# A macaron encoder layer: scale vectors of three RMS norms spread into PSUM by transposes, and the late norms moved to VectorE

## The chip, the cores and the metric

One core of one Trainium2 chip. The time is that of one execution on the device in microseconds; the number to predict is the median of several runs. A core has TensorE (matmul, "PE"), VectorE ("DVE"), ScalarE ("ACT"), GpSimd ("POOL") and SyncE ("SP", which here only issues DMAs). TensorE writes its results into PSUM, which has eight banks of 128 x 512 float32. VectorE and ScalarE read PSUM too. Each engine works through its own queue in order.

## The reference

One layer on x of 1024 tokens by 1024 channels, float32. An RMS norm multiplies each token by a number of its own and each channel by a learned scale vector (the "gain"):

```
x = x + 0.5 * swiglu(rms_norm(x, ffn1_norm), ffn1_wg, ffn1_wu, ffn1_wd)
x = x + hybrid_mixer(rms_norm(x, mix_norm), ...)      # Fourier branch and differential attention, gated
x = x + 0.5 * swiglu(rms_norm(x, ffn2_norm), ffn2_wg, ffn2_wu, ffn2_wd)
return rms_norm(x, final_norm)

rms_norm(x, g) = x * rsqrt(mean(x * x, over channels) + eps) * g
swiglu(x, wg, wu, wd) = (silu(x @ wg) * (x @ wu)) @ wd
```

## The kernel before

Tokens are cut into eight tiles of 128, t = 0 to 7; a tile is kept as two pieces of 128 tokens x 512 channels. Every float32 product is made of three reduced-precision ones, for which each operand is split in a high part (ScalarE, L133) and a low part (VectorE or GpSimd, L134). The large products use a seven-product scheme on 2 x 2 blocks (`seven_products`, L370): for each block of output columns TensorE runs seven products of twelve matmuls (L386) into two "p" banks of PSUM, ScalarE copies a product out (L398), VectorE adds another to the copy (L402). The weights of these products are loaded by SP into `r2` tiles, summed by GpSimd (L217) and split (L133, L134).

Each of the three norms feeds such products, so the normalized tokens must be turned (channels onto partitions), summed for the scheme, and split:

- `norm_tile` (L349) multiplies the two pieces of a tile in place by the token number r (a column) and the gain (128 x 512, the same row on every partition). One VectorE instruction does both products of a piece (L358). With `spread` the first piece goes another way: ScalarE multiplies by r (L355), GpSimd by the gain (L356).
- Two tiles make a pair. `pair_blocks` (L305) appends six steps to the list `blocks`: `first` turns two pieces (eight 128 x 128 transposes on TensorE, L295, into two "b" banks), `second` and `third` one piece each into one bank, with copies, sums (L312, L326, L334, L335) and splits of what lies in the banks; the three others split sums in SBUF. A bank is free again after the last of its readers.
- The gains are loaded by `load_gain` (L265): two DMAs, each of which reads 512 numbers and writes them onto 128 partitions, into two pieces of the store "x".

PSUM is dealt out as four "b" banks and four "p" banks. `bank()` takes the next "b" bank in turn; where `bank_list` holds banks, it deals those in rotation.

Where the norms run:

- Start (first norm): x is loaded tile by tile, with the gain's DMAs behind tile 1. Tiles 0 to 3 are normalized at once and their two pairs mostly turned before the first product. Tiles 4 to 7 come later: `each1` (L1131) is called after each of the first fourteen products, which work on tokens of tiles 0 to 3 alone (256 columns); its calls 4 to 7 normalize a tile each, the last two with `spread`, and each call takes one step (two from call 7 on) from `blocks` (`drain`).
- The second norm: the down projection before it (`Lower.run`) ends with the sums for tiles 4 to 7. Tiles 0 to 3 are normalized in `tail` (L624), while these products run, with banks that they leave free. `late` (L659) is called after each of the first fourteen products of the mixer (`project`); in its calls 1 to 4 it normalizes tiles 4 to 7, all with `spread`, by `done1`.
- The third norm: the same with `done2`, before the second feed-forward (`ffn`, with `each2`).

The order in each engine's queue is set when the program is built: a planner simulates the program with its own costs (`schedule_with_timeline_sim`, L2011) and places what is ready by program order; instructions marked `in_order` (in `norm_tile` from tile 4 on) are kept in program order.

Of the kernel before, what the change touches and what calls it, by code (L numbers as in the profile page):

```python
# [10 lines left out]
F32 = mybir.dt.float32  # L11
F32R = mybir.dt.float32r
I32 = mybir.dt.int32
AF = mybir.ActivationFunctionType
ALU = mybir.AluOpType
# [4 lines left out]
P = 128  # L20
S = 1024
D = 1024
DT = D // P
# [11 lines left out]
NP = NF // 2  # L35
SPILL = 5
# [12 lines left out]
def encoder_layer(ctx: ExitStack, tc: tile.TileContext, a: dict, out: bass.AP):  # L49
    nc = tc.nc  # L50
    pe, act, dve, pool, sp = nc.tensor, nc.scalar, nc.vector, nc.gpsimd, nc.sync

    cst = ctx.enter_context(tc.tile_pool(name="cst", bufs=1))
    big = ctx.enter_context(tc.tile_pool(name="big", bufs=1))
    dram = ctx.enter_context(tc.tile_pool(name="dram", bufs=1, space=DRAM))
    psum = [None]
# [13 lines left out]
    bank_list = []  # L70

    def bank(tag="b"):
        if bank_list:
            bank_list.append(bank_list.pop(0))
            return bank_list[-1]
        tag = tag if tag in banks else "b"
        return T(psum[0], tag, [P, 512], F32, banks[tag])
# [7 lines left out]
    def r2(shape=None, dt=F32):  # L85
        return T(big, "r2", shape or [P, 512], dt, 14)
# [20 lines left out]
    def give(piece):  # L107
        store[piece[0]].append(piece[1])
# [14 lines left out]
    ident = cst.tile([P, P], F32, name="ident")  # L123
# [132 lines left out]
    def drain(n, skip=()):  # L256
        while n > 0:
            due = [e for e in blocks if e[0] not in skip][:1]
            if not due:
                return  # L260
            blocks.remove(due[0])
            due[0][1]()
            n -= 1

    def load_gain(src):  # L265
        g = [take("x"), take("x")]
        for k in range(2):
            sp.dma_start(out=g[k][1],
                         in_=src[k * 512:(k + 1) * 512].rearrange("(o d) -> o d", o=1).broadcast_to([P, 512]))
        return g  # L270

    def squares(ss, k, xts, junk):

        for i, xt in enumerate(xts):
            src = xt if len(junk.shape) == 2 else xt.rearrange("p (j c) -> p j c", j=4)
            act.activation(junk, src, AF.Square, accum_out=ss[:, 4 * k + i:4 * k + i + 1])
# [69 lines left out]
    half_pair = {}  # L346
    few = [True]

    def norm_tile(t, x, gain, r, spread=False):  # L349

        for k in range(2):
            y = x[k][1]
            keep = in_order if t >= 4 else lambda ins: ins
            if spread and k == 0:
                act.activation(y, y, AF.Copy, scale=r)  # L355
                keep(pool.tensor_tensor(out=y, in0=y, in1=gain[k][1], op=ALU.mult))  # L356
            else:
                keep(dve.scalar_tensor_tensor(out=y, in0=y, scalar=r, in1=gain[k][1], op0=ALU.mult, op1=ALU.mult))  # L358
        half_pair[t] = x
        if t % 2 == 0:  # L360
            return
        pair_blocks(t // 2, half_pair.pop(t - 1), half_pair.pop(t))
# [261 lines left out]
    def tail(low, done):  # L624

        drains = DRAINS[len(low.units)]
        ss, r, turns = [], [], [0]
        few[0] = not low.spills

        def halves(t0, k):  # L630
            return [low.tile(t)[k][1] for t in range(t0, t0 + 4)]

        def hook(q, j, other):
            n = 2 - NBLK + q
            if n == -1 and j == 0:
                done(None, None, None)
                ss.extend((col(8), col(8)))
                low.ss = ss[1]
                ss.append(take("x"))
                squares(ss[0], 1, halves(0, 1), ss[2][1])  # L640
                act.activation(root, ss[0][:, 4:5], AF.Sqrt)
            if n < 0:
                return
            if n == 0 and j == 0:
                squares(ss[0], 0, halves(0, 0), ss[2][1])
                r.extend(rscale(ss[0]))
            if n == 1 and j == 1:
                squares(ss[1], 0, halves(4, 0), ss[2][1])
                give(ss[2])
            bank_list[:] = other[turns[0]:] + other[:turns[0]]  # L650
            if n == 0 and j < 4:
                done(j, low.tile(j), r[j])
            if (n, j) in drains:
                drain(drains[n, j], (T4,))
            turns[0] = other.index(bank_list[0])
            bank_list.clear()
        return hook

    def late(low, done):  # L659

        n, r = [0], []

        def hook():
            n[0] += 1
            if n[0] == 1:
                squares(low.ss, 1, [low.tile(t)[1][1] for t in range(4, TT)], spare(B11))
                r.extend(rscale(low.ss))
            if 1 <= n[0] <= 4:
                t = 3 + n[0]
                done(t, low.tile(t), r[t - 4])  # L670
            drain(1 if n[0] <= 4 else 2)
        return hook


# [23 lines left out]
    sums_d = {k: dram.tile([n, 4, P, 512], F32, name=f"sums{k}_d") for k, n in ((1, NP), (2, NP), ("o", 4))}  # L698

    def down(k, j):  # L700

        f = [a[f"ffn{k}_wd"][t * P:(t + 1) * P, :] for t in (j, j + NP)]
        return [f[i // 2][:, (i % 2) * 512:(i % 2) * 512 + 512] for i in range(4)]
# [9 lines left out]
    def right_sums(jobs):  # L713

        sub = ALU.subtract
        for blks, dst in jobs:
            two = [T(big, "kx", [P, 2, 512], F32, 2) for _ in range(2)]
            b = [t[:, q, :] for t in two for q in range(2)]
            for i in (1, 0, 3, 2):
                in_order(sp.dma_start(out=b[i], in_=blks[i]))  # L720
            for _ in range(4):
                yield
            t3 = rh()
            for n, (o, x, y) in enumerate(((t3, b[3], b[1]), (b[1], b[1], b[0]), (b[3], b[3], b[1]), (b[2], b[2], b[3]))):
                in_order(dve.tensor_tensor(out=o, in0=x, in1=y, op=sub))
                if n % 2 == 1:
                    yield
            for n, o in enumerate((b[1], b[3], t3, b[2])):
                in_order(sp.dma_start(out=dst[n], in_=o))
            yield  # L730
            yield
# [200 lines left out]
    x2_d = dram.tile([S, D], F32, name="x2_d")  # L932
# [160 lines left out]
    keep = {}  # L1093
# [13 lines left out]
    x0 = []  # L1107
    for t in range(TT):
        x0.append([take("h" if t < 4 else "x") for _ in range(2)])
        for k in range(2):  # L1110
            sp.dma_start(out=x0[t][k][1], in_=a["x"][t * P:(t + 1) * P, k * 512:(k + 1) * 512])
        if t == 1:
            gain = load_gain(a["ffn1_norm"])
        elif t == 3:
            ws.ahead(3, 0)
    for t in range(4):
        ss = col(2)
        for k in range(2):
            act.activation(bank(), x0[t][k][1], AF.Square, accum_out=ss[:, k:k + 1])
        r = rscale(ss)[0]  # L1120
        norm_tile(t, x0[t], gain, r)
        if t == 2:
            drain(1)
    drain(6)
    ss = col(8)
    for k in range(2):
        squares(ss, k, [x0[t][k][1] for t in range(4, TT)], spare(B22))
    r4 = rscale(ss)
    hooks = [0]

    def each1():  # L1131
        n = hooks[0]
        hooks[0] += 1
        if 4 <= n <= 7:
            norm_tile(n, x0[n], gain, r4[n - 4], n >= 6)
        if n == 7:
            for g in gain:
                give(g)
        drain(1 if n < 7 else 2)

    low = ffn(1, a["x"], each1, right_sums([(down(1, j), sums_d[1][j]) for j in (*range(SPILL, NP), *range(SPILL))]
                                           + [(outward(j), sums_d["o"][j]) for j in range(4)]), bias_prepare(), mixer_weights())
    state = {}

    def done1(t, x, r):
        if t is None:
            state["gain"] = load_gain(a["mix_norm"])
            ws.open()
            ws.ahead(ws.used + 3, ws.used)
            return  # L1150
        if t == 0:
            new_xn()
        for k in range(2):
            act.dma_start(out=x1_d[t * P:(t + 1) * P, k * 512:(k + 1) * 512], in_=x[k][1])
        norm_tile(t, x, state["gain"], r, t >= 4)

    low.run(tail(low, done1))

# [28 lines left out]
            project((h, 4 + h), None, cols, hook)  # L1189
        hook = None  # L1190
    assert not blocks
    for g in state["gain"]:
        give(g)
    rv = bias_general()
    psum_pool.__exit__(None, None, None)
    psum_pool = tc.tile_pool(name="psum2", bufs=1, space=PSUM, reuse_waits="tile")
# [629 lines left out]
    for n_, (dm, hh) in enumerate(todo):  # L1826
# [8 lines left out]
        y, gb = ready[n_]  # L1835
# [23 lines left out]
    def done2(t, x, r):  # L1859
        if t is None:  # L1860
            state["gain"] = load_gain(a["ffn2_norm"])
            ws.open()
            ws.ahead(ws.used + 3, ws.used)
            return
        if t == 0:
            new_xn()
        for k in range(2):
            act.dma_start(out=x2_d[t * P:(t + 1) * P, k * 512:(k + 1) * 512], in_=x[k][1])
        norm_tile(t, x, state["gain"], r, t >= 4)

    low.run(tail(low, done2))


    def each2():
        hook2()
        if hooks2[0] == 4:
            for g in state["gain"]:
                give(g)
        hooks2[0] += 1

    hook2, hooks2 = late(low, done2), [0]
    low = ffn(2, x2_d, each2, right_sums([(down(2, j), sums_d[2][j]) for j in (*range(SPILL, NP), *range(SPILL))]))

    def done3(t, x, r):
        if t is None:
# [137 lines left out]
```

## Time and profile before

| | us |
|---|---|
| median of 3 runs (2053.23 to 2053.57) | 2053.23 |
| the profiled execution, its own time | 2054.49 |
| its span, first to last instruction | 2052.7 |
| TensorE busy in the span | 1959.5 (95%) |
| VectorE busy | 1421.3 (69%) |
| ScalarE busy | 1002.1 (49%) |
| GpSimd busy | 649.7 (32%) |

The span is what the profile covers; the profiled execution took 1.8 us more than it. Busy shares are means over the whole span. The mean granted clock of TensorE is 0.981 of full speed.

### The profile page before, as it was taken

To read this page: it belongs to the slowest core of one execution; us is meant where nothing else is said; L and a number is where in the kernel's file an instruction comes from. 1 tells how busy PE (TensorE), PEld (TensorE's weight loads), DVE (VectorE), ACT (ScalarE), POOL (GpSimd) and SP (SyncE) were. 2 spreads that over 40 slices of the span, in tenths; PEclk is the share of its full clock that TensorE was granted. 3 is DMA by queue.
4 is the path that set the end of the run, shared out by engine and by line. 5 is a ranking of instruction groups with operands and counts; after the bars stand their busy time and mean duration, and the time that the engine had idled before them with its cause. 6 is when DMAs were issued, how large, how long until landed. Compare 5 with 4: busy or idle time off the path is not lost.

```text
span 2052.7 us, 27589 instructions
## 1 busy us (share of the span) xinstructions
PE 1959.5 (95%) x9433; PEld 1644.1 (80%) x9433; DVE 1421.3 (69%) x2152; ACT 1002.1 (49%) x1808; POOL 649.7 (32%) x487
## 2 busy tenths in 40 slices
PE   5899999999999999999998898997999999999998
PEld 4787888888888888888886786877888888888886
DVE  7867776648767765656657986769665654578765
ACT  6444444334445545867756753256433333344454
POOL 6623332320000454434364640057432323300010
PEclk9999999999999999999999899998999999999999
DMA  4466975419426444344358668431745432256335
GB/s 144 150 214 230 315 256 187 159 52 340 148 76 197 127 147 128 113 144 135 117 160 273 207 201 301 146 103 65 238 173 186 175 113 67 62 206 230 108 98 174
DMA packets 205455, 342.11 MB, mean 167 GB/s; under 512 B 22108, under 2 KB 63052, under 8 KB 204800
## 3 DMA queue, kind: packets, MB, share of 16 engines
q1 hardware_dynamic: 198032, 324.86, 48.1%
q10 hardware_dynamic: 5760, 12.59, 1.7%
q0 software_dynamic: 1520, 2.88, 0.5%
q8 instruction: 74, 1.21, 0.2%
q14 instruction: 69, 0.57, 0.1%
HBM read 250.04 MB, written 94.40 MB: 168 GB/s over the span
## 4 chain that ended last, share of the span: by engine, by line
PE 53%; DVE 4%; DMA 3%; issue 1%; POOL 1%; ACT 1%; SPq 0%; DVEq 0%; ACTq 0%; POOLq 0%
PE p L386 31%; PE b L588 9%; PE p L588 3%; PE A L1300 2%; PE b L1376 1%; PE b L1334 1%; PE p L1618 1%; DMA r<-proj_d 1%; PE b L1347 1%; PE b L1801 1%; DVE op L134 1%; DVE n L134 1%; DMA rh<-proj_d 0%; PE p L1801 0%; DVE h L358 0%
## 5 line engine op out<-in xcount | busy, mean ns | idle before, releaser
L386 PE MATMUL p<-n,op 128*128 128x512 f32 (+1 forms) x5256 | 1157.1, 380 | 30.6 <-DVE r L402 8.4
L386 PEld LDWEIGHTS p<-n,op 128*128 128x128 f32 x5256 | 951.6, 192 | 216.1 <-DVE r L402 8.0
L217 POOL TENSOR_TENSOR r<-r,r 128x512 f32<-128x512 f32 x252 | 363.0, 1447 | 881.4 <-DVE op L134 506.3
L134 DVE TENSOR_TENSOR op<-r,op 128x512 fp32r<-128x512 f32 x427 | 356.8, 840 | 290.2 <-ACT op L133 279.9
L133 ACT ACTIVATE op<-r 128x512 fp32r<-128x512 f32 x446 | 277.4, 627 | 294.4 <-PE p L386 201.6
L588 PE MATMUL b<-n 128*128 128x512 f32 x996 | 237.5, 391 | 0.9 <-DVE r L1836 0.9
L588 PEld LDWEIGHTS b<-n 128*128 128x128 f32 x996 | 187.3, 188 | 40.2 <-ACT op L133 1.3
L398 ACT ACTIVATE r<-p 128x512 f32<-128x512 f32 (+1 forms) x138 | 74.2, 537 | 130.0 <-PE p L386 130.0
L588 PE MATMUL b<-op,op 128*128 128x512 f32 x528 | 129.2, 391 | 2.7 <-DVE op L134 2.7
L588 PEld LDWEIGHTS b<-op,op 128*128 128x128 f32 x528 | 99.3, 189 | 23.7 <-DVE op L134 3.1
L402 DVE TENSOR_TENSOR r<-p,r 128x512 f32<-128x512 f32 (+1 forms) x138 | 84.6, 615 | 41.4 <-PE p L386 39.6
L133 ACT ACTIVATE n<-n 128x512 fp32r<-128x512 f32 x126 | 74.7, 621 | 66.8 <-PE b L588 23.3
L134 DVE TENSOR_TENSOR n<-n,n 128x512 fp32r<-128x512 f32 x118 | 82.4, 717 | 27.1 <-ACT n L133 27.0
L588 PE MATMUL p<-n 128*128 128x512 f32 x336 | 80.1, 390 | 0.0
L1895 POOL TENSOR_TENSOR r<-r,x 128x512 f32<-128x512 f32 x5 | 7.7, 1560 | 224.3 <-ACT r L1894 224.3
L588 PEld LDWEIGHTS p<-n 128*128 128x128 f32 x336 | 62.9, 188 | 12.9
L1318 POOL TENSOR_TENSOR x<-x,x 128x1024 f32<-128x1024 f32 x16 | 38.4, 2398 | 101.4 <-ACT x L1317 101.4
L588 PE MATMUL p<-op,op 128*128 128x512 f32 x288 | 68.3, 390 | 0.0
L588 PEld LDWEIGHTS p<-op,op 128*128 128x128 f32 x288 | 53.8, 188 | 11.0
L133 ACT ACTIVATE op<-n 128x512 fp32r<-128x512 f32 x66 | 39.3, 621 | 36.4 <-PE b L588 13.4
L1303 DVE CUSTOM_DVE_ANT_0 x<-A,x 128x1024 f32<-128x1024 f32 x32 | 39.0, 1219 | 21.2 <-PE b L1334 11.5
L133 ACT ACTIVATE n<-x 128x512 fp32r<-128x512 f32 x48 | 30.1, 631 | 43.8 <-PE b L588 32.9
(331 smaller groups left out, 2482.7 us busy)
## 6 DMA issues: line engine op xcount, KB each, us to landing
kx<-in_ffn_wd SPq DMA_DIRECT2D x118, 256.0 KB
r<-in_ffn_wg SPq DMA_DIRECT2D x96, 256.0 KB
r<-in_ffn_wu SPq DMA_DIRECT2D x94, 256.0 KB
n<-sums_d SPq DMA_DIRECT2D x88, 256.0 KB
sums_d<-kx SPq DMA_DIRECT2D x66, 256.0 KB
proj_d<-r SPq DMA_DIRECT2D x56, 256.0 KB
h_d<-x SPq DMA_DIRECT2D x16, 512.0 KB
rh<-proj_d SPq DMA_DIRECT2D x64, 128.0 KB
```

The lines of the kernel that those rows point to most:

```text
L133: act.activation(hi, src, AF.Copy)
L134: eng.tensor_tensor(out=lo, in0=src, in1=hi, op=ALU.subtract)
L217: pool.tensor_tensor(out=b[o], in0=b[x], in1=b[y], op=op)
L386: pe.matmul(ps, lhsT=w[wi][:, d * P:(d + 1) * P], rhs=xn[b][xi][:, d, cols], start=(first and m == 0), stop=(last and m == 11), skip_group ...
L398: act.activation(o, view(p), AF.Copy)
L402: dve.tensor_tensor(out=o, in0=view(p), in1=o, op=ALU.add)
L588: pe.matmul(ps[p], lhsT=wa[ai][:, p * P:(p + 1) * P], rhs=wb[bi], start=(j == 0 and m == 0 and name in self.FRESH), stop=False, skip_group ...
L1300: pe.matmul(ps[:, ns], lhsT=q[:, qs], rhs=kk[:, ns], start=(n == 0), stop=(n == 1))
L1303: dve.tensor_tensor_reduce(out=dst, in0=ps, in1=bt, scale=-0.125, scalar=3.0e38, op0=ALU.add, op1=ALU.min, accum_out=nmx)
L1318: pool.tensor_tensor(out=s1, in0=s2, in1=s1, op=ALU.add)
L1334: pe.transpose(pt[:, j * P:(j + 1) * P], s1[:, (4 * q + j) * P:(4 * q + j + 1) * P], ident)
L1347: pe.matmul(po[:, 0:2 * P], lhsT=vp, rhs=d[:, k, :], start=(n == 0), stop=(n == 3 * TT - 1))
```

## The change

- `gain_col` loads a gain of 1024 numbers as eight rows of 128 (4 KB), turns them by one transpose into 128 x 8, and copies that to SBUF. It is called for all three gains behind x tile 0, where `load_gain` had stood behind tile 1.
- `bank_gain` takes the four "b" banks. ScalarE writes each column of a gain 128 times side by side (two copies of 128 x 512, into two `r2` tiles), TensorE turns these by eight transposes, so that two banks hold the gain on every partition. The two other banks become `bank_list`. The gain stays in PSUM until the last norm that uses it; then `bank_list` is cleared.
- The first norm uses the PSUM gain for all eight tiles. The second and third use it for tiles 4 to 7; tiles 0 to 3 keep the loaded gain, whose two pieces are given back as soon as the down projection has ended.
- `spread` is gone: both pieces of each tile go to VectorE (L358).
- The late norms are called at every second product: after calls 4, 5, 7 and 9 in the start, after calls 1, 2, 4 and 6 in `late`. The calls that take two steps from `blocks` begin two later.
- The squares of x tiles 0 to 3 in the start write their unused output to "p" banks, not "b" banks.

```diff
     def bank(tag="b"):
-        if bank_list:
+        if bank_list and tag == "b":
...
+    def gain_col(key, src):
+
+        rows = r2([DT, P])
+        sp.dma_start(out=rows, in_=src.rearrange("(k p) -> k p", p=P))
+        pt = bank()
+        pe.transpose(pt[:, 0:DT], rows, ident[0:DT, 0:DT])
+        gain_cols[key] = cst.tile([P, DT], F32, name=f"gain_{key}")
+        dve.tensor_copy(out=gain_cols[key], in_=pt[:, 0:DT])
+
+    def bank_gain(key):
+
+        bs = [bank() for _ in range(4)]
+        wide = [r2(), r2()]
+        for k in range(2):
+            c = gain_cols[key][:, 4 * k:4 * k + 4].rearrange("p (j o) -> p j o", o=1)
+            act.activation(wide[k].rearrange("p (j c) -> p j c", j=4), c.broadcast_to([P, 4, P]), AF.Copy)
+            for j in range(4):
+                pe.transpose(bs[k][:, j * P:(j + 1) * P], wide[k][:, j * P:(j + 1) * P], ident)
+        bank_list[:] = bs[2:]
+        return [("psum", b) for b in bs[:2]]
...
-    def norm_tile(t, x, gain, r, spread=False):
+    def norm_tile(t, x, gain, r):
...
-            if spread and k == 0:
-                act.activation(y, y, AF.Copy, scale=r)
-                keep(pool.tensor_tensor(out=y, in0=y, in1=gain[k][1], op=ALU.mult))
-            else:
-                keep(dve.scalar_tensor_tensor(out=y, in0=y, scalar=r, in1=gain[k][1], op0=ALU.mult, op1=ALU.mult))
+            keep(dve.scalar_tensor_tensor(out=y, in0=y, scalar=r, in1=gain[k][1], op0=ALU.mult, op1=ALU.mult))
...
@@ late @@
-            if 1 <= n[0] <= 4:
-                t = 3 + n[0]
+            if n[0] in (1, 2, 4, 6):
+                t = 4 + n[0] // 2
                 done(t, low.tile(t), r[t - 4])
-            drain(1 if n[0] <= 4 else 2)
+            if n[0] == 6:
+                bank_list.clear()
+            drain(1 if n[0] < 7 else 2)
...
@@ start @@
-        if t == 1:
-            gain = load_gain(a["ffn1_norm"])
+        if t == 0:
+            for k in ("ffn1", "mix", "ffn2"):
+                gain_col(k, a[f"{k}_norm"])
+            gain = bank_gain("ffn1")
...
-            act.activation(bank(), x0[t][k][1], AF.Square, accum_out=ss[:, k:k + 1])
+            act.activation(bank("p"), x0[t][k][1], AF.Square, accum_out=ss[:, k:k + 1])
...
@@ each1 @@
-        if 4 <= n <= 7:
-            norm_tile(n, x0[n], gain, r4[n - 4], n >= 6)
-        if n == 7:
-            for g in gain:
-                give(g)
-        drain(1 if n < 7 else 2)
+        if n in (4, 5, 7, 9):
+            t = 4 + (n - 3) // 2
+            norm_tile(t, x0[t], gain, r4[t - 4])
+        if n == 9:
+            bank_list.clear()
+        drain(1 if n < 9 else 2)
...
@@ done1; done2 is changed in the same way, with bank_gain("ffn2") @@
-        norm_tile(t, x, state["gain"], r, t >= 4)
+        norm_tile(t, x, state["gain"], r)
 
     low.run(tail(low, done1))
+    for g in state["gain"]:
+        give(g)
+    state["gain"] = bank_gain("mix")
```

## Rows read from the trace of the kernel before

**Rows 1.** Page, part 1: busy us, share of the span, instructions.
```profile
PE 1959.5 (95%) x9433; PEld 1644.1 (80%) x9433; DVE 1421.3 (69%) x2152; ACT 1002.1 (49%) x1808; POOL 649.7 (32%) x487
```

**Rows 2.** Busy by stretch: us; PE, PEld, DVE, ACT, POOL (instructions); clock, DMA, GB/s.
```profile
28.00:80.00 52.00, 41.51 (x300) 39.70 (x299) 45.19 (x56) 28.84 (x60) 42.88 (x30) 0.93 0.19 61
694.00:716.00 22.00, 19.20 (x147) 18.68 (x146) 21.04 (x27) 13.50 (x31) 19.16 (x12) 0.92 0.37 118
1388.00:1412.00 24.00, 15.84 (x79) 14.60 (x78) 22.23 (x29) 16.70 (x35) 20.27 (x14) 0.74 0.19 66
...
1408.00:1412.00 4.00, 4.00 (x21) 4.00 (x21) 4.00 (x4) 1.01 (x2) 4.00 (x3) 0.50 0.00 0
734.00:738.00 4.00, 4.00 (x35) 4.00 (x35) 2.61 (x3) 1.65 (x3) 3.92 (x4) 1.00 0.39 131
```

**Rows 3.** TensorE's waits, 0 to 100 us: us in total, times, longest.
```profile
PE b L295 <- DVE h L358: 18.7, 2, 11.4
...
PE b L295 <- DVE n L134: 2.6, 1, 2.6
```

**Rows 4.** Timeline of the start: start us, us, engine, line; in brackets idle before.
```profile
8.73 0.75 DVE L358 SCALAR_TENSOR_TENSOR h<-h,col,x 128x512 f32<-128x512 f32 x1 [3.01 <-DMA x<-in_ffn_norm]
...
20.47 3.45 DVE L358 SCALAR_TENSOR_TENSOR h<-h,col,x 128x512 f32<-128x512 f32 x2
...
26.92 0.69 DVE L134 TENSOR_TENSOR n<-b,n 128x512 fp32r<-128x512 f32 x1
27.30 0.59 ACT L133 ACTIVATE n<-b 128x512 fp32r<-128x512 f32 x1
...
27.75 1.09 PE L295 MATMUL b<-ident,h 128*128 128x128 f32 x4 [2.57 <-DVE n L134]
...
28.49 5.60 PE L386 MATMUL p<-n,op 128*128 128x256 f32 x37
```

**Rows 5.** Timeline of the mixer's first products.
```profile
701.70 2.56 ACT L355 ACTIVATE x<-x,col 128x512 f32<-128x512 f32 x4 [0.30 <-DVE col L285]
701.70 0.75 DVE L358 SCALAR_TENSOR_TENSOR x<-x,col 128x512 f32<-128x512 f32 x1
702.37 4.12 DVE L358 SCALAR_TENSOR_TENSOR x<-x,col,x 128x512 f32<-128x512 f32 x3
...
704.83 0.50 PE L386 MATMUL p<-n,op 128*128 128x256 f32 x2 [1.26 <-ACT op L133]
...
706.87 4.20 PE L386 MATMUL p<-n,op 128*128 128x256 f32 x22 [1.53 <-DVE r L402]
707.58 3.42 POOL L356 TENSOR_TENSOR x<-x,x 128x512 f32<-128x512 f32 x2
...
708.42 3.13 DVE L134 TENSOR_TENSOR op<-r,op 128x512 fp32r<-128x512 f32 x2
...
710.90 1.91 PE L295 MATMUL b<-ident,x 128*128 128x128 f32 x16
```

**Rows 6.** Timeline of the second feed-forward's first products.
```profile
1399.38 6.82 DVE L358 SCALAR_TENSOR_TENSOR x<-x,col,x 128x512 f32<-128x512 f32 x4
...
1403.94 6.76 POOL L356 TENSOR_TENSOR x<-x,x 128x512 f32<-128x512 f32 x4
...
1406.86 7.39 PE L386 MATMUL p<-n,op 128*128 128x256 f32 x37 [3.57 <-DVE n L134]
```

**Rows 7.** Forms of line L882: duration ns min/median/max, first and last start us.
```profile
L882 DVE SCALAR_TENSOR_TENSOR r<-r,r x14: 407/624/1516, 58.8 to 1461.8; 128x256 f32<-128x256 f32 x14
L882 DVE SCALAR_TENSOR_TENSOR r<-r,p x2: 403/406/408, 70.5 to 1435.7; 128x256 f32<-128x256 f32 x2
```

**Rows 8.** VectorE's groups by form, 28 to 72 us: busy us, mean ns.
```profile
L358 DVE SCALAR_TENSOR_TENSOR x<-x,col,x 128x512 f32<-128x512 f32 x6 | 8.0, 1367 | 0.0
L134 DVE TENSOR_TENSOR n<-b,n 128x512 fp32r<-128x512 f32 x9 | 6.1, 679 | 0.3 <-ACT n L133 0.3
...
L134 DVE TENSOR_TENSOR op<-r,op 128x512 fp32r<-128x512 f32 x3 | 4.7, 1566 | 1.1 <-ACT op L133 1.1
```

More of the change, by code (lines that the diff above doesn't have):

```diff
@@ L270, in load_gain @@
         return g
+    gain_cols = {}
+    def gain_col(key, src):
[15 more added lines that the diff above has]
+        return [("psum", b) for b in bs[:2]]
     def squares(ss, k, xts, junk):
@@ L1191, in encoder_layer @@
     assert not blocks
-    for g in state["gain"]:
-        give(g)
     rv = bias_general()
@@ L1868, in done2 @@
             act.dma_start(out=x2_d[t * P:(t + 1) * P, k * 512:(k + 1) * 512], in_=x[k][1])
-        norm_tile(t, x, state["gain"], r, t >= 4)
+        norm_tile(t, x, state["gain"], r)
     low.run(tail(low, done2))
[L1874 to L1882, printed above, removed]
+    for g in state["gain"]:
+        give(g)
+    state["gain"] = bank_gain("ffn2")
+    low = ffn(2, x2_d, late(low, done2), right_sums([(down(2, j), sums_d[2][j]) for j in (*range(SPILL, NP), *range(SPILL))]))
     def done3(t, x, r):
```

## The prediction, made before the change was run

> **What bounds the kernel now.** I read the page first. TensorE is busy for 95% of the span and VectorE for 69% [rows 1], so over most of the run nothing that VectorE or GpSimd does can matter. Then I read the busy time by stretch, to find where TensorE is not full. Three of the places are where the norms that the change touches run: 28 to 80 us (41.51 of 52 us busy), 694 to 716 us (19.20 of 22) and 1388 to 1412 us (15.84 of 24) [rows 2]. In all three VectorE is nearly full (45.19, 21.04 and 22.23 us) and GpSimd almost as full [rows 2]. So there VectorE sets the pace, and the mean of 69% hides it. [...] The list of TensorE's waits and the timelines then say what it waited for: in the start the norms (L358) and the freeing of a bank [rows 3, 4]; in the mixer ScalarE and then VectorE's addition L402, both queued behind norms [rows 5]; in the second feed-forward a split on VectorE, queued behind four norms [rows 6]. After each place TensorE is full again for hundreds of us, so what is gained or lost there stays.
>
> **The price of a norm product with the gain in PSUM.** The trace does not have L358 with a PSUM operand. The nearest row is the same instruction at L882, half as long: with both tensors in SBUF it took 407 to 1516 ns, with one in PSUM 403 to 408 [rows 7]. The same is seen in splits between 28 and 72 us, GpSimd being busy: nine that read PSUM took 679 ns on average, three that read only SBUF 1566 [rows 8]. So two SBUF operands cost some 0.9 us more when GpSimd works beside them, and one PSUM operand removes that. I take 0.75 us, the undisturbed L358 [rows 4]; bounds are 0.68 (the splits) and 1.37, the mean of the disturbed ones [rows 8].
>
> [...]
>
> **Part by part.**
>
> *Start, up to the first product (28.49 us).* VectorE stood idle for 3.01 us before the first norm, waiting for the broadcast gain [rows 4]. The new way has a 4 KB load, a small transpose, a copy, two ScalarE copies (0.59 us, as a ScalarE split [rows 4]) and eight transposes; it starts one x tile sooner and no longer puts two broadcast transfers ahead of tiles 2 and 3. Bounds 0 and -3.0; I take -1.5, since the chain has five links. Tile 3's two products took 3.45 us [rows 4] and will take 1.5: -1.9 (bounds 0 and -2.1). Against this, only two banks rotate. Before, the last four transposes waited 2.57 us for the split that frees the fourth bank (26.92 + 0.69 us) [rows 4]; with two banks pair 1's second group waits for it, and the first product needs that group: transposes 1.09, ScalarE 0.59, VectorE 0.69, so 27.6 + 2.4 = 30.0 instead of 28.5, +1.5 (bounds 0, if other work is put in front, and +1.5). Net -1.9. The eleven transposes fall where TensorE waits anyway (18.7 us in two waits [rows 3]); without that cover they cost 1.3, at the price of sixteen in 1.91 us [rows 5].
>
> *Start, tiles 4 to 7.* Six products took 8.0 us on VectorE [rows 8]; eight at 0.75 are 6.0: -2.0 (bounds -2.6 and +3.0, eight at 0.68 and at 1.37). The two GpSimd products that leave disturb up to two VectorE operations by 0.9 each: -1.0 (0 to -1.8). Two rotating banks: `third` must wait until the bank of `first`'s second group is read; its readers in a row are three on ScalarE at 0.59 and two on VectorE at 0.68, 3.1 us, where sixteen transposes once ran without a pause [rows 5]. Products fill most of that, if they are queued in front; +1.0 (0 to +3.1). Net -2.0.
>
> *Mixer.* ScalarE loses four products (2.56 us), behind which the split stood that TensorE waited 1.26 us for [rows 5]; two copies come in, and these need only the gain column, so they can run earlier: -1.3 (0 to -1.3). The norms ahead of the addition L402 were 0.75 + 4.12 us [rows 5]; by program order six of the eight now stand there, 4.5 us: -0.4 (+1.1 if all eight do, -1.5 at the most, the wait). Four GpSimd products go; VectorE splits beside them took 3.13 us for two [rows 5]: up to four times 0.9, I take -1.5 of 3.6. Eight transposes: +1.0 (0 to +1.0, half of 1.91 [rows 5]). Two banks: +1.0 as before. Net -1.2.
>
> *Second feed-forward.* Four norms held VectorE for 6.82 us, and a split that TensorE waited 3.57 us for stood behind them [rows 6]. Four at 0.75 are 3.0, 3.8 less than before: -3.6, the wait (only -0.8 if all eight are queued ahead of the split). After the wait 37 matmuls took 7.39 us [rows 6]; at 35 in 4 us they take 4.2, so 3.2 us went to the clock, which fell after TensorE had stood idle: -1.4 (0 to -3.2), as other waits remain. GpSimd's 6.76 us [rows 6] go: -1.0 (0 to -3.6). Transposes +0.5 (0 to +1.0; TensorE has 8 us idle in this stretch [rows 2], some of it there). Two banks +1.0. Net -4.5.
>
> What costs nothing: the three small DMAs instead of two broadcast ones (VectorE's 3.01 us of idling covers them, included above), the squares' move to other banks (their output is read by nobody), the pieces given back earlier. The later calls for tiles 6 and 7 end one call later, still inside the fourteen; if the second half's products had to wait for it, that is one product, 1.4 us (12 x 4/35).
>
> Sum: -1.9 - 2.0 - 1.2 - 4.5 = -9.6 us. The profiled execution took 2054.5 (span 2052.7 and 1.8 around it), so 2044.9 for such an execution. The median of the runs is 1.3 lower: 2043.6.
>
> **Rivals.**
>
> *Only a shift of queues.* All eight norms stand in a row ahead of what TensorE waits for, since the token numbers come late and `in_order` keeps them together; the GpSimd gain is used up by weight sums that come forward. Then the start gives -1.9 and nothing after, the mixer -1.3 + 1.1 + 1.0 = +0.8, the second feed-forward -0.8 + 0.5 = -0.3: -1.4, 2051.8. For it: the four norms of the second feed-forward did run in one block [rows 6]. Against it: half of the calls are now spaced two products apart.
>
> *Two banks are too few (slower).* TensorE's queue is in order; if the transposes of `third` are placed ahead of products and their bank is not free, everything stops behind them. For it: before, sixteen ran in one go [rows 5], and a bank did hold up TensorE for 2.57 us [rows 4]. Against it: the planner knows of the banks. At the full 3.1 us at three places, with the clock lost behind each as in the second feed-forward (3.2), it costs 18.9; without my 3 x 1.0 the rest of the sum is -12.6, so +6.3: 2059.5. It decides from 4.2 us at each place.
>
> *More than I take.* Terms at their far bounds (gain -3.0, clock -3.2, GpSimd -1.8, -3.6, -3.6, and no wait for banks): -9.6 - 1.5 - 1.8 - 0.8 - 2.1 - 2.6 - 4.5 = -22.9. Half of that extra gives -16: 2037.
>
> **How the numbers follow.** Forecast 0.62, queues only 0.20, slower 0.12, more 0.06. A change of this kernel under 0.2% (4.1 us) can hardly be told from none. Faster: 0.62 + 0.06 = 0.68; same 0.20; slower 0.12. The likeliest case is 2043.6, its own range 2038 to 2049. The range that should hold the time, 2037 to 2054, takes in the queues-only case and leaves out most of the slower one and half of the larger gain.
>
> **What would show it.** L358 with a PSUM operand near 0.75 us beside a busy GpSimd; no ScalarE or GpSimd products of norms; the first product before 28.49 us; the waits of 1.26 and 3.57 us gone; TensorE fuller and its clock higher in the three stretches. Wrong, if L358 takes over 1 us, if TensorE's transposes wait for banks longer than 3 us, or if its waits for L402 and the splits keep their length.

## The result, and the profile after

The changed kernel takes 2035.04 us (median of four runs, 2033.28 to 2036.15), beside 2053.4 us for the kernel before on the same chip: a ratio of 0.990, 95% interval [0.9888, 0.9912]. It gained 18.4 us where I had forecast 9.6, and fell below the range. The profiled execution took 2035.7 us with a span of 2033.9, against 2052.7 before.

The page, part 1 (busy us, share, instructions):

```profile
PE 1953.8 (96%) x9460; PEld 1635.3 (80%) x9460; DVE 1409.7 (69%) x2165; ACT 1000.8 (49%) x1804; POOL 629.8 (31%) x477
```

VectorE's total fell by 11.6 us and GpSimd's by 19.9 [rows 1], hardly to be seen in the shares. The forms of the norm's product, after (duration min/median/max in ns, first and last start in us; `b` is the gain in PSUM, a second `x` the loaded one):

```profile
L377 DVE SCALAR_TENSOR_TENSOR x<-x,col,b x24: 734/736/747, 35.8 to 1394.3; 128x512 f32<-128x512 f32 x24
L377 DVE SCALAR_TENSOR_TENSOR h<-h,col,x x16: 734/746/1780, 626.2 to 1360.0; 128x512 f32<-128x512 f32 x16
...
L377 DVE SCALAR_TENSOR_TENSOR h<-h,col,b x8: 731/744/748, 7.0 to 19.3; 128x512 f32<-128x512 f32 x8
```

With the gain in PSUM the slowest of 32 products took 748 ns; with it in SBUF some of the same kernel's still took 1780. The price in my sum, 0.75 us, was right. Busy time by stretch after, in the three places of [rows 2], the two later ones moved along with the work (columns as there):

```profile
28.00:80.00 52.00, 46.59 (x351) 44.75 (x351) 44.61 (x65) 30.73 (x62) 41.17 (x29) 0.93 0.34 113
683.00:705.00 22.00, 21.39 (x174) 20.46 (x173) 20.96 (x33) 16.02 (x35) 15.12 (x11) 1.00 0.39 119
1377.00:1401.00 24.00, 19.06 (x154) 18.03 (x153) 23.58 (x38) 20.53 (x45) 16.11 (x13) 1.00 0.37 110
```

VectorE is as full as before in each, but does 65, 33 and 38 instructions where it did 56, 27 and 29, and TensorE follows it (351 matmuls for 300, 174 for 147, 154 for 79). To see what each place gave, I set marks that both kernels pass with the same work behind them. A "wide copy" is ScalarE's first 128x512 copy of a product (L398, after L417), where the products on half of the tokens are over.

| mark | before | after | shift | forecast by then |
|---|---|---|---|---|
| first product | 28.49 | 26.18 | -2.3 | -1.9 |
| first wide copy, first feed-forward | 93.1 | 83.6 | -9.5 | -3.9 |
| first store of x1 | 608.1 | 596.7 | -11.4 | -3.9 |
| first store of x2 (end of the mixer) | 1340.1 | 1328.0 | -12.1 | -5.1 |
| first wide copy, second feed-forward | 1454.4 | 1435.0 | -19.4 | -9.6 |
| end of the span | 2052.7 | 2033.9 | -18.8 | -9.6 |

So the first norm's late tiles gave 7.2 us (forecast 2.0), the mixer 0.7 (1.2), the second feed-forward 7.3 (4.5). A further 1.9 came between 93 and 608 us, where nothing was changed. Most of it is one wait behind the first mark, before:

```profile
99.66 0.72 PE L386 MATMUL p<-n,op 128*128 128x512 f32 x2 [2.54 <-DVE op L134]
```

After, TensorE runs through there (131 matmuls from 81.63 us on, 28.60 us without a wait). Most of the kernels below, some with the gain in SBUF, lose this time too (from the first wide copy to the store of x1 515.0 us before, 513.1 after, 512.5 with the gain in SBUF and all else as changed, 511.9 with the spacing alone), so it is not the operand's. Two executions of the changed kernel differ by 1.1 us at the store of x1 and 3.3 at the end, so single marks carry about that much.

Now the same work rather than the same length of time: first product to first wide copy, and store of x2 to the next wide copy. The kernel before:

```profile
28.49:93.12 64.63, 53.68 (x375) 50.78 (x374) 54.30 (x72) 34.95 (x73) 45.70 (x33) 0.92 0.32 103
1340.10:1454.39 114.29, 100.35 (x577) 89.42 (x576) 87.45 (x117) 65.19 (x139) 70.61 (x50) 0.91 0.34 114
```

After:

```profile
26.18:83.64 57.46, 51.91 (x374) 49.30 (x374) 50.07 (x72) 33.47 (x67) 43.75 (x31) 0.94 0.37 124
1328.00:1435.02 107.02, 95.61 (x585) 84.66 (x584) 83.55 (x119) 63.59 (x135) 67.46 (x47) 0.97 0.36 118
```

In the start VectorE does its 72 instructions in 4.2 us less; TensorE stands idle for 5.55 instead of 10.95 us and does as many matmuls in 1.8 us less, at a higher clock (0.92, then 0.94). In the second feed-forward VectorE is relieved of 3.9 us; TensorE idles 2.5 less, and its busy time falls by 4.7 although it does eight transposes more (granted clock 0.91, then 0.97). In both, the stretch is shorter by 1.7 to 1.9 us for each microsecond that VectorE is busy less. That is no fixed rate: two kernels below have 1.3 and the opposite sign.

TensorE's waits from 28 to 100 us after (us in total, times, longest) are 5.2 us; before, those from 28.4 to 93.1 us alone were 10.6:

```profile
PE p L405 <- DVE op L134: 3.5, 1, 3.5
PE p L405 <- DVE r L421: 1.1, 1, 1.1
PE p L405 <- DVE n L134: 0.6, 1, 0.6
```

The timeline after, at the three places (start us, us, engine, line; idle before in brackets):

```profile
7.02 1.60 DVE L377 SCALAR_TENSOR_TENSOR h<-h,col,b 128x512 f32<-128x512 f32 x2 [0.31 <-PE b L291]
...
24.20 2.00 PE L318 MATMUL b<-ident,h 128*128 128x128 f32 x8 [3.64 <-DVE n L134]
...
26.18 3.30 PE L405 MATMUL p<-n,op 128*128 128x256 f32 x13
...
683.65 0.60 PE L291 MATMUL b<-ident,r 128*128 128x128 f32 x4
...
689.26 4.04 DVE L377 SCALAR_TENSOR_TENSOR x<-x,col,b 128x512 f32<-128x512 f32 x6
...
694.55 0.66 PE L318 MATMUL b<-ident,x 128*128 128x128 f32 x4 [0.37 <-ACT x L340]
...
1387.86 4.03 DVE L377 SCALAR_TENSOR_TENSOR x<-x,col,b 128x512 f32<-128x512 f32 x6
...
1387.99 1.70 PE L405 MATMUL p<-n,op 128*128 128x256 f32 x12 [0.89 <-DVE n L134]
```

The first norm product starts 1.7 us earlier than in [rows 4]. The gain's transposes in the mixer (683.65) run without a wait. In both later places six products still stand in a row on VectorE, as the rival of the shifted queues said, but they take 4.0 us, and TensorE's waits of 1.26 and 1.53 us [rows 5] and of 3.57 us [rows 6] are gone; the longest left are 0.37 among the mixer's first products (680 to 710 us), for a copy of ScalarE's, and in the second feed-forward 2.5 for a split of ScalarE's, where 2.3 stood before. The 0.89 is for another split, which stands ahead of the six products. One of my signs of being wrong did come: the transposes ahead of the first product waited 3.64 us for the split that frees their bank, longer than 3 us; the first product still came 2.3 us earlier.

### The profile page after: what moved, and what is told of

It is laid out like the page before. It is cut to its first block, busy times and chain, and to the rows that moved or that the text cites. A ratio compares the mean times of both kernels' runs of the same rounds, so it can differ in the third digit from the quotient of the medians.

```text
span 2033.9 us, 27633 instructions
## 1 busy us (share of the span) xinstructions
PE 1953.8 (96%) x9460; PEld 1635.3 (80%) x9460; DVE 1409.7 (69%) x2165; ACT 1000.8 (49%) x1804; POOL 629.8 (31%) x477
## 5 line engine op out<-in xcount | busy, mean ns | idle before, releaser
L417 ACT ACTIVATE r<-p 128x512 f32<-128x512 f32 (+1 forms) x138 | 74.1, 537 | 124.3 <-PE p L405 121.6
L607 PEld LDWEIGHTS p<-n 128*128 128x128 f32 x336 | 62.9, 188 | 13.0
L133 ACT ACTIVATE op<-n 128x512 fp32r<-128x512 f32 x66 | 39.3, 621 | 35.3 <-PE b L607 13.9
```

What stands on the lines that cost most here:

```text
L133: act.activation(hi, src, AF.Copy)
L417: act.activation(o, view(p), AF.Copy)
L607: pe.matmul(ps[p], lhsT=wa[ai][:, p * P:(p + 1) * P], rhs=wb[bi], start=(j == 0 and m == 0 and name in self.FRESH), stop=False, skip_group ...
```

## The experiments

My theory after the result was that the operand in PSUM carries the gain, since an instruction of VectorE with two SBUF operands and one of GpSimd slow each other (by themselves, below, the two took 1732 ns for 748 and 1681 for 1269). The rivals: the spacing of the late norms; the removal of ScalarE's and GpSimd's products; the earlier gain and first product. Beside the first four, the kernel before took 2054.18 us. Marks and stretches are read from one profiled execution of each kernel.

**The gain in SBUF, all else as changed.** The changed kernel with loaded gains and four banks:

```diff
-            gain = bank_gain("ffn1")
+        if t == 1:
+            gain = load_gain(a["ffn1_norm"])
...
-    state["gain"] = bank_gain("mix")
```

> The changed kernel with the gains loaded into SBUF by broadcast DMAs as before; all late norms on VectorE and at every second product, as changed. If the operand in PSUM carries the gain (contention between VectorE and GpSimd), the late L358 takes 1.2 to 1.8 us and nearly all is lost: 2048 to 2056 us. If taking the norms off ScalarE and GpSimd and spacing them carries it: 2033 to 2040. If the earlier gain and the lighter DMA at the start carry it: the start loses its 11 us and the second feed-forward keeps its 7: about 2046.

Measured: 2051.6 us, ratio 0.9991 [0.9980, 1.0001]. All on VectorE and spaced, but from SBUF, the change is worth 4 us at most by the interval. The products of tiles 4 to 7 in the start, then the stretches from first product to first wide copy and from the store of x2 to the next wide copy:

```profile
L377 DVE SCALAR_TENSOR_TENSOR x<-x,col,x 128x512 f32<-128x512 f32 x8 | 11.8, 1511 | 0.0
...
28.52:91.40 62.88, 52.15 (x371) 49.36 (x370) 55.94 (x74) 33.79 (x72) 45.82 (x33) 0.95 0.35 117
...
1337.60:1454.31 116.71, 100.89 (x582) 88.63 (x581) 91.06 (x120) 63.45 (x136) 69.78 (x48) 0.93 0.35 119
```

The products took 1.51 us on average. In the start VectorE is busy 1.6 us longer than before, and the stretch is 1.75 us shorter all the same. In the second feed-forward the wait of 3.57 us is gone here too (the longest left for such a split is 0.62), and yet the stretch is 2.4 us longer than before: TensorE waits elsewhere (it idles for 15.8 us of this stretch, before for 13.9).

**The spacing alone.** The kernel before with the late norms at every second product, ScalarE and GpSimd as they were:

```diff
-        if 4 <= n <= 7:
-            norm_tile(n, x0[n], gain, r4[n - 4], n >= 6)
...
+        if n in (4, 5, 7, 9):
+            t = 4 + (n - 3) // 2
+            norm_tile(t, x0[t], gain, r4[t - 4], t >= 6)
```

> The kernel before with the late norms at every second product and nothing else changed. If the operand in PSUM carries the gain: within 4 us of 2053.4. If the spacing is a large part: 2040 to 2048, above all through the second feed-forward, where four norms in one block held up a split for 3.57 us.

Measured: 2053.24 us, ratio 1.0 [0.9990, 1.0009]. Nothing, to within 2 us. The first store of x1 came at 604.1, 4.0 us earlier than before, and none of that was left at the end; so this mark alone proves little.

**The start alone.** The first norm as changed, the two others as before (the lines against the changed kernel):

```diff
-        norm_tile(t, x, state["gain"], r)
+        norm_tile(t, x, state["gain"], r, t >= 4)
```

> The kernel before with the new start alone (one gain in PSUM, all eight tiles on VectorE, spaced); the second and third norm as before. If the three places add up as the two traces put it (first product of the mixer 11.4 us sooner), 2042 us. If the places hang on one another, or the planner sets the rest of the program differently, more than 2 us off that.

Measured: 2044.07 us, ratio 0.9955 [0.9938, 0.9972], some 9 to 10 us; the 2042 of the sum is inside the interval. First wide copy at 83.2 us, in an execution (2038.29 us) that was 5.5 us faster than any other of this kernel.

**The gain copied out of PSUM.** The changed kernel, but ScalarE copies the two banks of gain to SBUF, and four banks rotate again:

```diff
-        return [("psum", b) for b in bs[:2]]
+            act.activation(g[k][1], bs[k], AF.Copy)
+        return g
```

> The changed kernel, but each PSUM gain is copied by ScalarE to SBUF (two copies of 128 x 512 for each of three gains) and the norms read it there; no bank is held, four banks rotate. The gain still comes without broadcast DMAs. If the operand in PSUM carries the change: 2046 to 2054, a little under e1_gain_in_sbuf by the earlier start (2.3 us at the first product). If the early gain and the lighter DMA carry the start: 2036 to 2042, with the first product of the mixer still some 10 us sooner than before.

Measured: 2053.09 us, ratio 0.999 [0.9979, 1.0002]. Where the product reads the gain is what differs from the change, with four banks for two and six copies more on ScalarE, and the gain of time is gone. But the total says less than it seems. The start still came out ahead: first product 25.95, first wide copy 87.7 us, which is 5.4 of the changed kernel's 9.5, so a part of the start's gain does not need the operand. And the mixer lost 9 us against the kernel before; why so much I did not find out. The second feed-forward up to its wide copy took 115.3 us, no less than before.

The next four ran against 2053.76 us.

**Two banks alone.** The kernel before, two rotating banks in all three norms:

```diff
+            bank_list[:] = [bank(), bank()]
```

> The kernel before, with the gains loaded and the products as they were, but with two rotating banks for the norms' transposes in all three norms instead of four (the squares write to the banks of the products). This is what my prediction charged with 1.5 + 1.0 + 1.0 + 1.0 us. If that charge is right, the time rises by 3 to 5 us, to 2057 to 2059, and the first product comes at 29 to 30 us instead of 28.49. If two banks cost nothing (the planner puts other work between), the time is within 2 us of before. The rival 'two banks are too few' gives over 8 us more, as splits that wait behind the slow products of before hold a bank longer.

Measured: 2053.33 us, ratio 1.0004 [0.9993, 1.0016], so -1.4 to +3.3 us. The 4.5 us that I charged for it are outside. TensorE does wait for a bank, as its timeline shows:

```profile
27.53 1.97 PE L295 MATMUL b<-ident,h 128*128 128x128 f32 x8 [5.04 <-DVE n L134]
29.34 3.65 PE L386 MATMUL p<-n,op 128*128 128x256 f32 x13
```

The first product comes 0.85 us late, the first wide copy 1.7 and the store of x1 0.8; at the store of x2 nothing is left of it.

**Early tiles of the start alone.** Tiles 0 to 3 read PSUM, tiles 4 to 7 the loaded gain in the old way:

```diff
+            gain0 = bank_gain("ffn1")
+        elif t == 1:
             gain = load_gain(a["ffn1_norm"])
```

> The first norm alone, and of it only tiles 0 to 3: their products read the gain from PSUM; tiles 4 to 7 take it from the loaded copy, spread over ScalarE, GpSimd and VectorE at the old places, with four banks; mixer and second feed-forward as before. Theory A (the late tiles carry the start, since their products stand in VectorE's queue beside a busy GpSimd): the first product comes near 26 us, the first wide copy of the second column block near 91, and the time falls by 2 to 3 us, to about 2051. Theory B (an early first product lets the whole start run further ahead): the time falls by 8 to 11 us, as with the whole start changed, to about 2044.

Measured: 2052.14 us, ratio 0.9996 [0.9985, 1.0008]. From its first product to its first wide copy:

```profile
25.54:93.60 68.06, 55.27 (x374) 52.84 (x375) 54.45 (x74) 36.54 (x77) 47.00 (x34) 0.90 0.29 94
```

The first product is 2.95 us earlier than before and the first wide copy half a microsecond later: TensorE stands idle 1.8 us longer in between, and is busy 1.6 us longer at a lower clock (0.90 for 0.92). Theory B is out. Theory A's 2 to 3 us lie within the interval (-3.1 to +1.6 us), but the wide copy, which it put near 91, shows none of them.

**The two later norms alone.**

```diff
+            gain = load_gain(a["ffn1_norm"])
...
-            gain = bank_gain("ffn1")
```

> The second and the third norm alone: their late tiles' products read the gain from PSUM and stand at every second product; the first norm as before. If the gains of the three places add up, this is the change less the start alone: about -7 to -8 us, 2046 to 2047, of which 0 to -1.5 us in the mixer and -6 to -7 in the second feed-forward, first x1 store within 1 us of 608.1. If the later places only gain because the start has put them otherwise (clock or the weights' transfers), less than 3 us is left.

Measured: 2046.39 us, ratio 0.997 [0.9956, 0.9983], -7.4 us by the medians: the mixer took 2.7 us less, the second feed-forward up to its wide copy 7.5. With the start's 9 to 10 us this makes 15 to 17 of the 18.4: the places add up, within the intervals.

**PSUM in the tails too.** The changed kernel with the PSUM gain also for tiles 0 to 3 of the second and third norm (filled into two banks that the down projection leaves free):

```diff
+                if key is not None:
+                    state["gain"] = fill_gain(wide, other)
...
-    low.run(tail(low, done1))
...
+    low.run(tail(low, done1, "mix"))
```

> The changed kernel, with the gain in PSUM also for the first four tiles of the second and third norm, which still read a loaded copy in the changed kernel (two banks that the tail doesn't need are filled with the gain at its start; the two broadcast loads go). If two SBUF operands beside a busy GpSimd are what costs, eight products in each tail fall from about 1.3 to 0.75 us, and where TensorE waits behind them up to 2.7 us come back at the third norm: 2 to 5 us less than the changed kernel. If TensorE is covered in these stretches by the products of the down projection, no change (within 2 us).

Measured: 2032.34 us, ratio 0.9889 [0.9864, 0.9915]. Its second feed-forward up to the wide copy took 104.75 us instead of 107.02, its mixer 735.6 instead of 731.3. Whether the whole is faster than the changed kernel the times do not show: the intervals overlap.

The next four ran against 2055.7 us.

**The product by itself.** A kernel of its own: 16 products with the gain in SBUF and 16 with it in PSUM, with GpSimd idle and beside a chain of its additions, in one execution.

> Nothing of the layer is computed: a kernel of its own, which times the norm's product (128x512, one scalar column, in place) on VectorE 16 times with the gain in SBUF and 16 times with it in PSUM, first with GpSimd idle, then beside a chain of GpSimd additions of two SBUF tiles; 12 of these additions also run alone. If the pairing of two SBUF operands with a busy GpSimd is the cause: about 0.75 us for both kinds with GpSimd idle, 1.4 to 1.8 us for the SBUF kind beside it and still 0.74 for the PSUM kind; and GpSimd's addition longer beside the first kind than beside the second. [...] If the slow products of the full kernel come from something else there (DMA writes, TensorE), both kinds stay near 0.75 us here.

Its VectorE groups (busy us, mean ns): L46 and L48 with GpSimd idle, L56 and L58 beside it:

```profile
L56 DVE SCALAR_TENSOR_TENSOR x<-x,col,g 128x512 f32<-128x512 f32 x16 | 26.6, 1732 | 0.0
L46 DVE SCALAR_TENSOR_TENSOR x<-x,col,g 128x512 f32<-128x512 f32 x16 | 11.0, 748 | 3.8 <-DMA x<-in_x 3.7
L48 DVE SCALAR_TENSOR_TENSOR x<-x,col,b 128x512 f32<-128x512 f32 x16 | 10.6, 742 | 0.0
L58 DVE SCALAR_TENSOR_TENSOR x<-x,col,b 128x512 f32<-128x512 f32 x16 | 10.6, 735 | 0.0
```

GpSimd's additions of two SBUF tiles alone (L43), then beside the SBUF kind (x17) and beside the PSUM kind (x9):

```profile
L43 POOL TENSOR_TENSOR u<-u,v 128x512 f32<-128x512 f32 x11 | 13.5, 1269 | 0.0
...
L51 POOL TENSOR_TENSOR u<-u,v 128x512 f32<-128x512 f32 x17 | 28.0, 1681 | 0.1
...
L51 POOL TENSOR_TENSOR u<-u,v 128x512 f32<-128x512 f32 x9 | 11.5, 1317 | 0.0
```

Without GpSimd the operand's place makes no difference to speak of (748 ns in SBUF, 742 in PSUM); beside it the SBUF kind takes 1.0 us more, the PSUM kind nothing, and GpSimd's addition is slowed too, by 0.41 us.

**The operand without the spacing.** The changed kernel with the late tiles at the old calls:

```diff
-        if n in (4, 5, 7, 9):
-            t = 4 + (n - 3) // 2
+        if 4 <= n <= 7:
+            t = n
```

> The changed kernel with the late tiles at the old calls, one in each of four successive products, in all three norms (gain in PSUM, two banks, all on VectorE). If the PSUM operand carries the gain by itself, the time stays within 3 us of the changed kernel, 2033 to 2038. If the spacing is needed as well (eight products in a row, 6 us, ahead of the splits and of the addition in VectorE's queue), it gives back 3 to 8 us, 2038 to 2043, with waits of TensorE of 3 us and more in the mixer and in the second feed-forward.

Measured: 2033.93 us, ratio 0.9892 [0.9868, 0.9916]. For the total, the spacing is not needed; the first wide copy came at 85.4 instead of 83.6 us.

**The changed kernel again, and with PSUM in the third norm's tail alone.** These two ran on the same chip:

```diff
-    low.run(tail(low, done2))
...
+    low.run(tail(low, done2, "ffn2"))
```

> The changed kernel once more, on the same chip as the next run, so that the two can be compared: 2033 to 2038 us.

> The changed kernel with the gain in PSUM also for the first four tiles of the third norm only; with both later norms changed so, the second feed-forward took some 4 us less by its milestones and the mixer some 4 us more. If both are the edit's, this run keeps the gain without the loss: 3 to 5 us less than the changed kernel in the same call. If these are the scatter from one schedule to another, it is within 3 us of it.

Measured: 2033.7 us (2030.76 to 2036.14), ratio 0.9898 [0.9879, 0.9917], and 2031.35 us (2030.26 to 2032.23), ratio 0.9884 [0.9863, 0.9904]. The second feed-forward up to the wide copy took 104.87 us in the second kernel, as with both tails changed (104.75), against 107.02 and 107.21 in two executions of the changed kernel. So the tail gives 2.2 us there, less than the 3 to 5 that I expected of the edit; the times fit, but their intervals overlap. The mixer's 4 us of loss did not come back (731.6 us); whether the mixer's own tail costs them stays open, as mixers differ by as much without any edit (below). It is the fastest version here, by a margin that the times alone do not settle.

Two more, against 2054.59 us, ask where the start's gain sits.

**Late tiles of the start alone.** Tiles 0 to 3 from the loaded gain, tiles 4 to 7 as changed:

```diff
+    gain4 = bank_gain("ffn1")
...
+            norm_tile(t, x0[t], gain4, r4[t - 4])
```

> The complement of the run on the early tiles: of the first norm only tiles 4 to 7 are as in the changed kernel (gain in PSUM, all on VectorE, every second product, two banks); tiles 0 to 3 read the loaded gain with four banks, and mixer and second feed-forward are as before. If the error of my forecast sits in the late tiles of the start, the first product comes near 28.5 us and the first x1 store still 7 to 9 us before 608.1, at 599 to 601, and the time falls by 6 to 9 us. If the start needs both (the early first product puts the late tiles in front of other work), the store moves by under 4 us.

Measured: 2050.05 us, ratio 0.9981 [0.9971, 0.9992], 1.6 to 6.0 us and so less than I expected. First wide copy at 89.5, x1 at 601.8 us; the first product came at 31.8, not near 28.5.

**The operand of six products alone.** Late tiles at the old calls, the two pieces of ScalarE and GpSimd as before, only VectorE's six products from PSUM:

```diff
+            norm_tile(n, x0[n], [gain[0], gain4[1]] if n >= 6 else gain4, r4[n - 4], n >= 6)
```

> As the run before, but the late tiles stand at the old calls, one in each of four successive products, and the first halves of tiles 6 and 7 are still scaled by ScalarE and multiplied by GpSimd with the loaded gain: only the operand of the six products on VectorE is in PSUM. VectorE is relieved of about 3.6 us there (six at 1.37 become six at 0.74, less 0.2 of scatter). If the operand is the cause by itself, the first x1 store comes 3 to 6 us before 608.1; if taking the two products from GpSimd or the spacing is needed for it, by under 2 us.

Measured: 2050.28 us, ratio 0.998 [0.9970, 0.9991]. x1 at 599.8 us, 8.3 earlier than before where I expected 3 to 6, though the spacing alone moved this mark by 4.0 for nothing. From first product to first wide copy:

```profile
30.80:87.50 56.70, 50.66 (x377) 48.83 (x376) 48.07 (x71) 35.25 (x73) 46.98 (x33) 0.94 0.38 125
```

Six operands moved to PSUM (with two banks and the gain's transposes, which they need), and this stretch falls from 64.6 to 56.7 us; GpSimd keeps its two products. VectorE is busy 6.2 us less, so here the stretch is shorter by 1.3 us for each. But the first product comes 2.3 us late (30.80 us), and that can shorten the stretch too (below): the wide copy comes 5.6 us earlier, of the 9.5 in the changed kernel, and the whole gains 4 (1.8 to 6.2).

The start, in twelve of the kernels (us; length is from the first product to the first wide copy):

| kernel | first product | first wide copy | length |
|---|---|---|---|
| before | 28.5 | 93.1 | 64.6 |
| two banks alone | 29.3 | 94.8 | 65.5 |
| spacing alone | 28.8 | 92.2 | 63.4 |
| all changed but gain loaded | 28.5 | 91.4 | 62.9 |
| gain copied out of PSUM | 26.0 | 87.7 | 61.7 |
| early tiles alone | 25.5 | 93.6 | 68.1 |
| two later norms alone | 31.0 | 94.4 | 63.4 |
| late tiles alone | 31.8 | 89.5 | 57.7 |
| operand of six products alone | 30.8 | 87.5 | 56.7 |
| PSUM, old calls | 25.4 | 85.4 | 60.0 |
| start alone | 26.1 | 83.2 | 57.1 |
| changed | 26.2 | 83.6 | 57.5 |

With the late tiles' gain in PSUM the length is 57 to 60, without it 62 to 68. A late first product shortens it by some: with the two later norms alone, where no product of the start is changed, the first product came 2.5 us later than before and the length was 1.2 less.

The later places, over all kernels: from the store of x2 to the next wide copy it took 104.8 to 107.7 us in the six executions in which the late tiles of the third norm read PSUM, and 113.1 to 116.7 in the nine in which they read SBUF, whatever was done to spacing and banks. From the store of x1 to that of x2, the mixer, it took 729.3 to 735.6 us with PSUM, and 729.6 to 735.2 in the five kernels whose mixer is as before. So the second feed-forward's gain is the operand's, and for the mixer no gain is shown.

## Why the prediction was wrong

The direction was right, and so were the price of a product and its reason. What failed is how a relief of VectorE was turned into time. Step by step:

- *The price of a norm product*: 0.75 us forecast, 0.736 measured, and the reason [rows 7, 8] holds in the isolated run: beside GpSimd 1732 ns with the gain in SBUF and 735 with it in PSUM, without it 748 and 742.
- *Start, up to the first product*: -1.9 forecast, -2.3 measured. But I added it as if it stood by itself. With the old late tiles an earlier first product was worth nothing (early tiles alone: -2.95 us there, +0.5 at the wide copy); with the late tiles in PSUM it was worth all of itself: from the late tiles alone to the whole start the first product moves by 5.6 us and the wide copy by 5.9.
- ***Start, tiles 4 to 7*: the step that failed.** I took -2.0 (eight products at 0.75 for six at 1.37), -1.0 for GpSimd's disturbance and +1.0 for banks: -2.0. I took a microsecond of VectorE for one of the end, and had no term for the clock there. It was -7.2. VectorE was relieved of 4.2 us: the norm products gave 2.5 (8.0 us busy before, 5.5 after), other operations 1.7 on balance, some faster (three `h<-r,h` from 1739 to 1396 ns), but the splits `op<-r,op` slower (952 to 1087 ns). Against these 4.2 us, TensorE's 10.95 us of idling fell by 5.4 and its busy time by 1.8, on the same matmuls. VectorE itself stood idle for 10.3 us of the stretch before and for 7.4 after, so it was not the whole pace either. And a part is not the operand's: with the gain copied out of PSUM and the rest as changed, the length still fell by 2.9.
- *Two banks*: charged with 1.5, 1.0, 1.0 and 1.0; two banks alone cost -1.4 to +3.3 in all. I had priced a wait of TensorE as a delay of the end. TensorE did wait, and up to the first wide copy 1.7 us of it stayed; by the store of x2 it was made up. What made it up is not shown.
- *Mixer*: -1.2 forecast, -0.7 measured, -2.5 and -2.7 in two other executions with the same edit. The waits of 1.26 and 1.53 us went as I said, but no gain is shown: with the start alone changed, the mixer took 2.4 us less too, and with the early tiles alone 3.2 more. TensorE was idle for 34.5 us of the mixer's 732.0 before; so it was not full behind this place, as I had said, and what is gained ahead of it need not stay.
- *Second feed-forward*: -4.5 forecast, -7.3 measured. I had tied -3.6 to one wait. It went, but it went with the gain in SBUF too, where nothing was gained: the wait was not what the operand gives back. Over the whole stretch TensorE's idling fell by 2.5 us, and in a second execution by 3.3. The other term that was too small is the clock: -1.4, taken from one wait's aftermath (37 matmuls [rows 6] against the pace of 35 in 4 us at a clock of 1.00 [rows 2]), where the busy time of the stretch fell by 4.7 (3.8 in the second execution) in spite of eight more transposes, at a granted clock of 0.97 (0.95) instead of 0.91.
- *What costs nothing*: the later calls cost nothing, as I said, and the old ones would have done as well.
- *Rivals*: "only a shift of queues" saw the row of six products rightly, but at 0.7 us each they no longer hurt. "Two banks are too few" did not come about. "More than I take", which got 0.06, named two terms rightly (no cost of banks, clock at its far bound) and reached 2037.

That a relief of VectorE returns more than itself through waits and clock is read from the stretches; the parts of TensorE's clock and of its waits were not separated by a run of their own.

## What to carry to other kernels

Where VectorE and GpSimd work side by side, try one operand of VectorE's two-tensor instructions in PSUM: it cost two banks and eight transposes per gain here. It saved 1.0 us for each instruction beside an unbroken chain of GpSimd's additions, and 0.4 for each of these additions; in the layer's start it was 0.8 for each instruction (1.51 us with the gain loaded, 0.74 with it in PSUM). Price a relief of a busy engine over the whole stretch, by what the fed engine loses there in idle time and lost clock together, and not by the instruction or by one wait. Where the operand was moved, a stretch became shorter by 1.3 to 1.9 us for each of VectorE's; that is a reading of these stretches, not a rate. And don't add up terms in a row of waits: here a first product 2.95 us earlier was worth nothing as long as the late tiles were slow, two banks charged with 4.5 us cost 3.3 at most, and a wait of 3.57 us went without any gain.

## What the chip showed that I had not expected

The slowing is mutual: beside products with two SBUF operands GpSimd's addition took 1681 ns on average instead of 1269, and VectorE's product 1732 instead of 748; I had counted VectorE's loss only. And in that run the product was not slower with the gain in PSUM, 735 to 742 ns against 748 with it in SBUF and GpSimd idle.
